# A layer of a hybrid decoder on one core: numbered banks in two lead-ins, another order of the cross attention, and four output weights split ahead

## The chip, the cores and the metric

The kernel runs on one core of a Trainium2 chip. The time is that of one execution on the device in microseconds; of several executions the median counts. Four compute engines work beside each other, each through its own queue in order: TensorE (PE in the profile) multiplies matrices into PSUM, which has eight banks of 512 fp32 values in each of 128 partitions; VectorE (DVE), ScalarE (ACT) and GpSimd (POOL) do the rest. SyncE (SP) issues nearly all DMA transfers. Semaphores order what the queues do.

## The reference, cut

One layer, 1024 tokens of 1024 features in fp32. First comes a token mixer (attention, a state-space branch, gates), then cross attention into 256 memory tokens, then a gated feed-forward network; each with an RMS norm before and after, added to the stream. What lies around the change:

```
h = rms_norm(x, g_pre_xa)
q = (h @ w_xq).reshape(bsz, seq, 4, 256)
k, v = split(mem_n @ w_xkv)                      # 256 memory tokens, 4 heads of 256
s = einsum('bshd,bmhd->bhsm', q, k) * 256 ** -0.5
p = softmax(s, axis=-1)
o = einsum('bhsm,bmhd->bshd', p, v).reshape(bsz, seq, 1024)
x = x + rms_norm(o @ w_xo, g_post_xa)
h = rms_norm(x, g_pre_ffn)
gate, up = split(h @ w_gu)                       # start of the feed-forward network
```

## The kernel before

Nearly every product is made of three: an operand is split into a high part, rounded to the fast fp32 format of TensorE, and the low part that is left, and `mm3` sums high x high, high x low and low x high. So a split costs one copy (`hi_sb`, on GpSimd or ScalarE in turn) and one subtraction (`lo_of`, on VectorE unless told otherwise).

The tokens are taken in two halves of 512 and in eight chunks of 128. The two big products h @ w_xq and h @ w_gu are made by a Strassen scheme on quadrants. `opening` (L1603) makes the first two products of such a scheme while the norm of the last row chunk still runs, in the banks of the pools psa (`bank`) and psx (`two_banks`, tile p). `lead_in` (L1619) goes on: `first_sum` on VectorE adds the first two products (into qT in the cross attention, into t in the feed-forward network), the pool psx is closed, and a pool psl with six banks opens in its place. Which of the six a tile gets is decided by the pool: all of them have the name mm. na[0] and na[1] are the next two products, banks[4:6] take the transposes of the last row chunk (`late.pop()`), pb the two after that.

The cross attention (L1790 to L1837) works on one chunk of 128 queries at a time in `soft`: scores of four heads into a tile p of two banks, a maximum (VectorE), four exponentials with their sums (ScalarE), reciprocal and multiplication (VectorE). `turn_(half, h)` transposes the probabilities of one head and four chunks (`tr`) and splits them (pTh on ScalarE, pTl on VectorE). `mix(half, h)` multiplies them with the values (xk holds these, split) into one of two banks, and splits the result (h). The loop turns a step ahead of the mix, and puts the scores of chunks 4 to 7 between the first mixes. In this part the program's own scheduler decides the order in each engine's queue.

`big_weight` fetches the eight row blocks k0 to k7 of w_xo into two rooms (wraw) and splits them into bw0 to bw7, once the queries (qT) are done. `out_proj` multiplies chunk by chunk with them (L125 to L127 of `mm3`, tile p), normalises, adds to the stream, and normalises again; a chunk's two banks become free when VectorE has read them (L1457).

A class `InTurn` (L34) stands before TensorE, VectorE and ScalarE: between `in_turn(True)` and `in_turn(False)` each instruction of such an engine is put behind the one before it in the code. Instructions recorded in that way all have the line L49. The lead-ins are inside such a stretch.

Of the kernel before, what the change touches and what calls it, by code (L numbers as in the profile page):

```python
# [54 lines left out]
def hybrid_block(ctx, tc, a, out, dbg=None):  # L55
# [1309 lines left out]
    def big_weight(wb, w, npool=0, raw_on_top=False):  # L1365
# [5 lines left out]
        first = [] if raw_on_top else [raw_room()]  # L1371
        rooms = {k: mk(wb, [P, 2, D], F32R, f"bw{k}", bufs=1) for k in reversed(range(KT))}
        for k in range(KT):
            raw = first.pop() if first else raw_room()
            nc.sync.dma_start(raw, w[k * P:(k + 1) * P, :])
            both = rooms[k]
            wh.append(both[:, 0, :])
            wl.append(both[:, 1, :])
            hi_sb(wh[k], raw, "p" if k < npool else None)
            lo_of(wl[k], raw, wh[k], G if k < npool else V)  # L1380
# [227 lines left out]
    def lead_in(hb, xf, pa, pb, q, nq, sfp, swp, y, n00, ny, last, nlast, open_ps, open_tx, loaded):  # L1608
# [56 lines left out]
        banks = [mk(psl, [P, HALF], F32, "mm") for _ in range(6)]  # L1665
# [64 lines left out]

    with ExitStack() as q2:
        qp = pool(q2, "qp", side="right")
        qP = [mk(qp, [P, 2, S], F32, f"qT{f}") for f in range(KT // 2)]
# [11 lines left out]
        with ExitStack() as xs:  # L1745
# [8 lines left out]
            def open_ps():  # L1754
                psx.close()
                return pool(psl, "psl", 6, PSUM)
# [15 lines left out]
            psx = ExitStack()  # L1772
            psp = pool(psx, "psx", 2, PSUM)
        pp = pool(q2, "pp", 4, side="right")
        prp = pool(q2, "prob", 6, side="right")
# [11 lines left out]

        sc = 256.0 ** -0.5
        prob = {}

        def soft(c):
            pt = prob[c] = mk(prp, [P, 4, ML], F32, "prob")
            mx = mk(stats, [P, 4], F32, "mx", bufs=4)
            sm_ = mk(stats, [P, 4], F32, "sm", bufs=4)
            pscr = mk(psp, [P, 4, ML], F32, "p2")
            for h in range(4):
                for k in range(2):
                    T.matmul(pscr[:, h, :], qT[2 * h + k][:, c * P:(c + 1) * P], kT[:, 2 * h + k, :], start=k == 0, stop=k == 1)  # L1798
            V.tensor_reduce(mx, pscr, mybir.AxisListType.X, ALU.max)
            V.tensor_scalar(mx, mx, -sc, None, ALU.mult)  # L1800
            for h in range(4):
                A.activation(pt[:, h, :], pscr[:, h, :], AF.Exp, scale=sc, bias=mx[:, h:h + 1], accum_out=sm_[:, h:h + 1])
            V.reciprocal(sm_, sm_)
            V.tensor_tensor(pt, pt, sm_.unsqueeze(2).to_broadcast([P, 4, ML]), ALU.mult)
# [3 lines left out]
        def turn_(half, h):  # L1808
            for mt in range(2):
                pt = mk(psp, [P, HALF], F32, "tr")  # L1810
                for ci in range(4):
                    T.transpose(pt[:, ci * P:(ci + 1) * P], prob[half * 4 + ci][:, h, mt * P:(mt + 1) * P], ident)
                hi, lo = mk(pp, [P, HALF], F32R, "pTh"), mk(pp, [P, HALF], F32R, "pTl")
                A.activation(hi, pt, AF.Copy)
                V.tensor_tensor(lo, pt, hi.bitcast(F32), ALU.subtract)
                pT[half, h, mt] = hi, lo

        def mix(half, h, out):
            for d in range(2):
# [4 lines left out]
                hi, lo = out[kk // 4]  # L1824
                A.activation(hi[:, kk % 4, :], po, AF.Copy)
                V.tensor_tensor(lo[:, kk % 4, :], po, hi[:, kk % 4, :].bitcast(F32), ALU.subtract)

        ox = [quad(h2, "h2"), quad(h2, "h2")]
        for c in range(4):
            soft(c)  # L1830
        steps = [(half, h) for half in range(2) for h in range(4)]
        turn_(0, 0)
        for i, (half, h) in enumerate(steps):
            if half == 0:
                soft(4 + h)
            if i + 1 < len(steps):
                turn_(*steps[i + 1])  # L1837
            mix(half, h, ox[half])

    q3, q3w = ExitStack(), ExitStack()  # L1840
    gpool = pool(q3, "gx3")
    wbig = pool(q3w, "wbigB", 8, side="right")
    wxo = big_weight(wbig, a["w_xo"][0], 2, True)
# [22 lines left out]
    with ExitStack() as q4:  # L1866
# [33 lines left out]
        def open_ps():  # L1900
            psx.close()
            return pool(psl, "psl", 6, PSUM)
# [299 lines left out]
```

## Time and profile before

| | |
|---|---|
| median of 3 runs | 2533.23 us (2532.54 to 2536.23) |
| profiled execution | 2529.46 us, span 2527.7 us |
| TensorE busy | 2452.0 us, 97% |
| VectorE, ScalarE, GpSimd busy | 1802.7, 1164.9, 818.6 us |
| mean granted TensorE clock | 0.996 |

The profile lists instructions with engine, line of the kernel, operation, and the tile that is written and those that are read. "[2.29 <-DVE qT L49]" behind a row says that its engine stood idle for 2.29 us before, and what ended that: an instruction of VectorE that writes qT, from line 49. A row of a timeline begins with its start and its length in microseconds; xN joins N neighbours. A matmul is shown with its whole passage through the array, so neighbours overlap, and their pace is read from their starts. PEld is the loading of weights into TensorE.

### The profile page before, as it was taken

To read this page: it belongs to the slowest core of one execution; us is meant where nothing else is said; L and a number is where in the kernel's file an instruction comes from. 1 tells how busy PE (TensorE), PEld (TensorE's weight loads), DVE (VectorE), ACT (ScalarE), POOL (GpSimd) and SP (SyncE) were. 2 spreads that over 40 slices of the span, in tenths; PEclk is the share of its full clock that TensorE was granted. 3 is DMA by queue.
4 is the path that set the end of the run, shared out by engine and by line. 5 is a ranking of instruction groups with operands and counts; after the bars stand their busy time and mean duration, and the time that the engine had idled before them with its cause. 6 is when DMAs were issued, how large, how long until landed. Compare 5 with 4: busy or idle time off the path is not lost. (4 is left out here: it accounts for less than half of the span.)

```text
span 2527.7 us, 33384 instructions
## 1 busy us (share of the span) xinstructions
PE 2452.0 (97%) x12306; PEld 2013.9 (80%) x12306; DVE 1802.7 (71%) x2165; ACT 1164.9 (46%) x2075; POOL 818.6 (32%) x638
## 2 busy tenths in 40 slices
PE   7999999999999999989999999999999999999998
PEld 5788888888788778877787778887788888888877
DVE  7765877767587877689889665566468555566997
ACT  5333455555456665566545313344335333334343
POOL 3221645443111211246556150101112322324662
PEclk9999999999999999999999999999999999999999
DMA  7441443333543444265332571321232323224232
GB/s 247 157 126 54 139 143 100 100 109 100 150 111 90 111 107 100 82 205 191 110 99 81 163 249 64 136 67 51 100 134 71 96 76 96 80 92 159 100 133 100
DMA packets 249133, 295.62 MB, mean 117 GB/s; under 512 B 17023, under 2 KB 169096, under 8 KB 248842
## 3 DMA queue, kind: packets, MB, share of 16 engines
q1 hardware_dynamic: 248682, 292.45, 37.0%
q8 instruction: 97, 1.59, 0.3%
q10 hardware_dynamic: 288, 1.05, 0.1%
q14 instruction: 66, 0.54, 0.1%
HBM read 202.20 MB, written 74.45 MB: 109 GB/s over the span
## 5 line engine op out<-in xcount | busy, mean ns | idle before, releaser
L911 DVE TENSOR_TENSOR_SCAN n<-n,mask 128x128 f32<-128x128 f32 (+7 forms) x128 | 189.8, 1509 | 23.8 <-ACT n L910 22.6
L122 DVE TENSOR_TENSOR sw<-sf,sw 128x512 fp32r<-128x512 f32 x142 | 127.4, 901 | 70.2 <-ACT sw L119 68.1
L119 ACT ACTIVATE sw<-sf 128x512 fp32r<-128x512 f32 x142 | 88.9, 628 | 155.8 <-PE mm L230 139.1
L928 ACT ACTIVATE wth<-tr,mone 128x512 fp32r<-128x512 f32 x192 | 110.7, 585 | 84.6 <-PE tr L925 82.6
L929 DVE SCALAR_TENSOR_TENSOR wtl<-tr,wth 128x512 fp32r<-128x512 f32 x192 | 99.6, 543 | 49.7 <-ACT wth L928 49.6
L196 POOL TENSOR_TENSOR sf<-wr,wr 128x512 f32<-128x512 f32 x36 | 52.4, 1455 | 235.5 <-DMA wr<-in_w_gu_dram 92.1
L693 DVE SCALAR_TENSOR_TENSOR b<-b,prmT,b 128x1023 f32<-128x1023 f32 (+2 forms) x72 | 109.6, 1522 | 16.9 <-ACT b L687 16.3
L122 DVE TENSOR_TENSOR sw<-wr,sw 128x512 fp32r<-128x512 f32 x107 | 100.1, 937 | 24.4 <-ACT sw L119 24.1
L115 POOL TENSOR_SCALAR v<-va 128x512 fp32r<-128x512 f32 x16 | 20.5, 1283 | 287.5 <-PE av L938 167.3
L229 PE MATMUL mm<-h,sw 128*128 128x512 f32 x288 | 112.0, 389 | 0.0
L230 PE MATMUL mm<-h,sw 128*128 128x512 f32 x288 | 111.7, 389 | 0.0
L228 PE MATMUL mm<-h,sw 128*128 128x512 f32 x288 | 109.9, 389 | 0.0
L910 ACT ACTIVATE n<-sc 128x512 f32<-128x512 f32 (+1 forms) x192 | 88.6, 494 | 46.1 <-PE tr L925 28.7
L173 POOL TENSOR_SCALAR rstd<-ms 128x1 f32<-128x1 f32 x74 | 29.2, 394 | 240.8 <-ACT x L180 164.6
L125 PE MATMUL mm<-oth,bw 128*128 128x512 f32 x256 | 104.3, 408 | 2.2 <-DVE a L1250 2.2
L125 PE MATMUL p<-bw,h 128*128 128x512 f32 x256 | 98.9, 392 | 2.4 <-DVE x L1457 2.4
L126 PE MATMUL mm<-otl,bw 128*128 128x512 f32 x256 | 101.2, 395 | 0.0
L127 PE MATMUL mm<-oth,bw 128*128 128x512 f32 x256 | 101.2, 395 | 0.0
L127 PE MATMUL p<-bw,h 128*128 128x512 f32 x256 | 100.2, 392 | 0.5 <-DVE h L122 0.5
L126 PE MATMUL p<-bw,h 128*128 128x512 f32 x256 | 100.0, 391 | 0.0
L925 PE MATMUL tr<-ident,n 128*128 128x128 f32 x576 | 95.4, 274 | 4.0 <-DVE wtl L929 4.0
L199 POOL TENSOR_TENSOR sf<-wr,sf 128x512 f32<-128x512 f32 x36 | 57.8, 1607 | 107.5 <-issue 85.6
(672 smaller groups left out, 7929.1 us busy)
## 6 DMA issues: line engine op xcount, KB each, us to landing
wr<-in_w_in_dram SPq DMA_DIRECT2D x36, 512.0 KB
wr<-in_w_gu_dram SPq DMA_DIRECT2D x72, 256.0 KB
zr<-in_w_in_dram SPq DMA_DIRECT2D x28, 512.0 KB
wraw<-in_w_in_dram SPq DMA_DIRECT2D x20, 512.0 KB
gu_d<-t SPq DMA_DIRECT2D x36, 256.0 KB
zs_d<-zo SPq DMA_DIRECT2D x32, 256.0 KB
xs_d<-b SPq DMA_DIRECT2D x32, 256.0 KB
kl<-gt SPq DMA_DIRECT2D x64, 128.0 KB
```

What stands on the lines that cost most here:

```text
L122: eng.tensor_tensor(o, i, hi.bitcast(F32), ALU.subtract)
L125: first = T.matmul(ps, sh, mh, start=start, stop=False)
L126: T.matmul(ps, sh, ml, start=False, stop=False)
L127: T.matmul(ps, sl, mh, start=False, stop=stop)
L228: T.matmul(ps, w[0][:, k, :], bh, start=first and k == 0, stop=False, skip_group_check=True)
L229: T.matmul(ps, w[0][:, k, :], bl, start=False, stop=False, skip_group_check=True)
L230: ins = T.matmul(ps, w[1][:, k, :], bh, start=False, stop=last and k == 3, skip_group_check=True)
L693: V.scalar_tensor_tensor(acc[:, sh:], y[:, :S - sh], cw(3 - sh, f), acc[:, sh:], ALU.mult, ALU.add)
L911: V.tensor_tensor_scan(nt[:, 0:L][:, ::-1], nt[:, 0:L][:, ::-1], mask[:, S - L:][:, ::-1], 1.0, ALU.mult, ALU.max)
L925: T.transpose(pt[:, tb * P:(tb + 1) * P], ns_[tb][:, i * P:(i + 1) * P], ident)
L928: A.activation(wh[:, t0 * P:], pt[:, t0 * P:], AF.Identity, bias=mone)
L929: V.scalar_tensor_tensor(wl[:, t0 * P:], pt[:, t0 * P:], -1.0, wh[:, t0 * P:].bitcast(F32), ALU.add, ALU.subtract)
```

## The change

- The six banks of both lead-ins have names of their own, mm0 to mm5, one buffer each.
- The cross attention is written in the order in which TensorE, VectorE and ScalarE are to take it, inside `in_turn(True)`. Scores go into four tiles of one bank (sc), two heads each. Probabilities have eight rooms, four tiles a8 of two chunks each. The multiplication with the reciprocal (`normed`) comes after the first half of the next chunk's maxima, or after a turn or a mix. Two turns are made ahead of the mixes; scores of chunks 6 and 7 stand between them. The split transposed probabilities live in tiles sw and pT.
- k0 to k3 of w_xo are fetched and split on GpSimd, high and low part, before the scores; k4 to k7 get the rooms of the queries and are split on ScalarE and VectorE after the last mix. The queries' pool lives on for them.
- `big_weight` loses two options that only w_xo used.

```diff
@@ -1362,13 +1362,13 @@
-    def big_weight(wb, w, npool=0, raw_on_top=False):
+    def big_weight(wb, w):
         wh, wl = [], []
...
-        first = [] if raw_on_top else [raw_room()]
+        first = [raw_room()]
         rooms = {k: mk(wb, [P, 2, D], F32R, f"bw{k}", bufs=1) for k in reversed(range(KT))}
@@ -1376,8 +1376,8 @@
             wl.append(both[:, 1, :])
-            hi_sb(wh[k], raw, "p" if k < npool else None)
-            lo_of(wl[k], raw, wh[k], G if k < npool else V)
+            hi_sb(wh[k], raw)
+            lo_of(wl[k], raw, wh[k])
         return wh, wl
@@ -1662,7 +1662,7 @@
         psl = open_ps()
-        banks = [mk(psl, [P, HALF], F32, "mm") for _ in range(6)]
+        banks = [mk(psl, [P, HALF], F32, f"mm{i}") for i in range(6)]
         pb, na = banks[0:2], banks[2:4]
@@ -1728,9 +1728,10 @@
+    q3w = ExitStack()
+    qp = pool(q3w, "qp", side="right")
     with ExitStack() as q2:
-        qp = pool(q2, "qp", side="right")
-        qP = [mk(qp, [P, 2, S], F32, f"qT{f}") for f in range(KT // 2)]
+        qP = [mk(qp, [P, 2, S], F32, f"bw{4 + f}") for f in range(KT // 2)]
         qT = [qP[f // 4 * 2 + f % 2][:, f % 4 // 2] for f in range(KT)]
@@ -1753,7 +1754,7 @@
                 psx.close()
-                return pool(psl, "psl", 6, PSUM)
+                return pool(psl, "psl", 1, PSUM)
@@ -1769,10 +1770,9 @@
             psl.close()
-            psx = ExitStack()
-            psp = pool(psx, "psx", 2, PSUM)
-        pp = pool(q2, "pp", 4, side="right")
-        prp = pool(q2, "prob", 6, side="right")
+        psm = pool(q2, "psm", 2, PSUM)
+        wbig = pool(q3w, "wbigB", 1, side="right")
+        ptp = pool(q2, "pT", 2)
         kT = mk(xk, [P, KT, ML], F32, "xk2")
@@ -1785,62 +1785,94 @@
+        wxo = [mk(wbig, [P, 2, D], F32R, f"bw{k}") for k in reversed(range(KT // 2))][::-1]
+
+        def xo_weight(k, hi_eng, lo_eng):
+            raw = mk(wbig, [P, D], F32, "wraw", 2)
+            nc.sync.dma_start(raw, a["w_xo"][0][k * P:(k + 1) * P, :])
+            hi_sb(wxo[k][:, 0], raw, hi_eng)
+            lo_of(wxo[k][:, 1], raw, wxo[k][:, 0], lo_eng)
+
+        for k in range(KT // 2):
+            xo_weight(k, "p", G)
+
         sc = 256.0 ** -0.5
-        prob = {}
+        pbt = [mk(accp, [P, 2, 4, ML], F32, "a8") for _ in range(NCH // 2)]
+        prob = [pbt[c // 2][:, c % 2] for c in range(NCH)]
+        sums, todo = {}, []
+
+        def normed():
+            while todo:
+                c = todo.pop()
+                V.reciprocal(sums[c], sums[c])
+                V.tensor_tensor(prob[c], prob[c], sums[c].unsqueeze(2).to_broadcast([P, 4, ML]), ALU.mult)
...
         def soft(c):
-            pt = prob[c] = mk(prp, [P, 4, ML], F32, "prob")
             mx = mk(stats, [P, 4], F32, "mx", bufs=4)
-            sm_ = mk(stats, [P, 4], F32, "sm", bufs=4)
-            pscr = mk(psp, [P, 4, ML], F32, "p2")
-            for h in range(4):
-                for k in range(2):
-                    T.matmul(pscr[:, h, :], qT[2 * h + k][:, c * P:(c + 1) * P], kT[:, 2 * h + k, :], start=k == 0, stop=k == 1)
-            V.tensor_reduce(mx, pscr, mybir.AxisListType.X, ALU.max)
-            V.tensor_scalar(mx, mx, -sc, None, ALU.mult)
-            for h in range(4):
-                A.activation(pt[:, h, :], pscr[:, h, :], AF.Exp, scale=sc, bias=mx[:, h:h + 1], accum_out=sm_[:, h:h + 1])
-            V.reciprocal(sm_, sm_)
-            V.tensor_tensor(pt, pt, sm_.unsqueeze(2).to_broadcast([P, 4, ML]), ALU.mult)
+            sums[c] = mk(stats, [P, 4], F32, "sm", bufs=4)
+            for h2 in range(2):
+                ps = mk(psm, [P, 2, ML], F32, "sc", 4)
+                for j in range(2):
+                    h = 2 * h2 + j
+                    for k in range(2):
+                        T.matmul(ps[:, j, :], qT[2 * h + k][:, c * P:(c + 1) * P], kT[:, 2 * h + k, :], start=k == 0, stop=k == 1)
+                m = mx[:, 2 * h2:2 * h2 + 2]
+                V.tensor_reduce(m, ps, mybir.AxisListType.X, ALU.max)
+                V.tensor_scalar(m, m, -sc, None, ALU.mult)
+                for j in range(2):
+                    h = 2 * h2 + j
+                    A.activation(prob[c][:, h, :], ps[:, j, :], AF.Exp, scale=sc, bias=mx[:, h:h + 1], accum_out=sums[c][:, h:h + 1])
+                if h2 == 0:
+                    normed()
+            todo.append(c)
...
             for mt in range(2):
-                pt = mk(psp, [P, HALF], F32, "tr")
+                pt = mk(psm, [P, HALF], F32, "tr")
                 for ci in range(4):
                     T.transpose(pt[:, ci * P:(ci + 1) * P], prob[half * 4 + ci][:, h, mt * P:(mt + 1) * P], ident)
-                hi, lo = mk(pp, [P, HALF], F32R, "pTh"), mk(pp, [P, HALF], F32R, "pTl")
-                A.activation(hi, pt, AF.Copy)
-                V.tensor_tensor(lo, pt, hi.bitcast(F32), ALU.subtract)
-                pT[half, h, mt] = hi, lo
-
-        def mix(half, h, out):
+                t = mk(ptp, [P, 2, HALF], F32R, "pT") if h % 2 else mk(ld, [P, 2, HALF], F32R, "sw")
+                A.activation(t[:, 0], pt, AF.Copy)
+                V.tensor_tensor(t[:, 1], pt, t[:, 0].bitcast(F32), ALU.subtract)
+                pT[half, h, mt] = t[:, 0], t[:, 1]
+            normed()
+
+        def mix(half, h):
             for d in range(2):
...
                     mm3(po, vh[mt][:, kk * P:(kk + 1) * P], vl[mt][:, kk * P:(kk + 1) * P], *pT[half, h, mt], mt == 0, mt == 1)
-                hi, lo = out[kk // 4]
+                hi, lo = ox[half][kk // 4]
                 A.activation(hi[:, kk % 4, :], po, AF.Copy)
                 V.tensor_tensor(lo[:, kk % 4, :], po, hi[:, kk % 4, :].bitcast(F32), ALU.subtract)
+                normed()
...
         ox = [quad(h2, "h2"), quad(h2, "h2")]
-        for c in range(4):
+        in_turn(True)
+        for c in range(6):
             soft(c)
+        turn_(0, 0)
+        soft(6)
+        turn_(0, 1)
+        soft(7)
         steps = [(half, h) for half in range(2) for h in range(4)]
-        turn_(0, 0)
-        for i, (half, h) in enumerate(steps):
-            if half == 0:
-                soft(4 + h)
-            if i + 1 < len(steps):
-                turn_(*steps[i + 1])
-            mix(half, h, ox[half])
-
-    q3, q3w = ExitStack(), ExitStack()
+        for i, step in enumerate(steps):
+            mix(*step)
+            if i + 2 < len(steps):
+                turn_(*steps[i + 2])
+        wxo += [mk(qp, [P, 2, D], F32R, f"bw{k}") for k in range(KT // 2, KT)]
+        for k in range(KT // 2, KT):
+            xo_weight(k, "a", V)
+        in_turn(False)
+    wxo = [w[:, 0] for w in wxo], [w[:, 1] for w in wxo]
+
+    q3 = ExitStack()
+    psx = ExitStack()
+    psp = pool(psx, "psx", 2, PSUM)
     gpool = pool(q3, "gx3")
-    wbig = pool(q3w, "wbigB", 8, side="right")
-    wxo = big_weight(wbig, a["w_xo"][0], 2, True)
     gpost, gpre = load_gain(gpool, "g_post_xa"), load_gain(gpool, "g_pre_ffn")
@@ -1899,7 +1931,7 @@
             psx.close()
-            return pool(psl, "psl", 6, PSUM)
+            return pool(psl, "psl", 1, PSUM)
```

VectorE's queue, where the first mixes of the cross attention and the last multiplications of probabilities stand, before (pTl: low part of transposed probabilities; h: that of a mix's result; sm: sums of a chunk; prob: its probabilities):

```order
L1826 TENSOR_TENSOR h_3200_15963<-mm_16162,h_3199_15962 128x512
L1826 TENSOR_TENSOR h_3200_15963<-mm_16171,h_3199_15962 128x512
L1815 TENSOR_TENSOR pTl_16206<-tr_16200,pTh_16205 128x512
L1803 RECIPROCAL sm_16182<-sm_16182 128x4
L1804 TENSOR_TENSOR prob_16180<-prob_16180,sm_16182 128x1024
L1815 TENSOR_TENSOR pTl_16215<-tr_16209,pTh_16214 128x512
L1803 RECIPROCAL sm_16238<-sm_16238 128x4
L1804 TENSOR_TENSOR prob_16236<-prob_16236,sm_16238 128x1024
L1826 TENSOR_TENSOR h_3202_15965<-mm_16218,h_3201_15964 128x512
L1826 TENSOR_TENSOR h_3202_15965<-mm_16227,h_3201_15964 128x512
L1815 TENSOR_TENSOR pTl_16262<-tr_16256,pTh_16261 128x512
L1815 TENSOR_TENSOR pTl_16271<-tr_16265,pTh_16270 128x512
```

and with the change (pT and sw: transposed probabilities, a: probabilities, sc: scores, h: result of a mix):

```order
L49 TENSOR_TENSOR pT_16167<-tr_16162,pT_16167 128x512
L49 TENSOR_TENSOR pT_16175<-tr_16170,pT_16175 128x512
L49 RECIPROCAL sm_16143<-sm_16143 128x4
L49 TENSOR_TENSOR a_3210_15985<-a_3210_15985,sm_16143 128x1024
L49 TENSOR_REDUCE mx_16180<-sc_16182 128x2
L49 TENSOR_SCALAR mx_16180<-mx_16180 128x2
L49 TENSOR_REDUCE mx_16180<-sc_16191 128x2
L49 TENSOR_SCALAR mx_16180<-mx_16180 128x2
L49 TENSOR_TENSOR h_3212_15987<-mm_16200,h_3211_15986 128x512
L49 RECIPROCAL sm_16181<-sm_16181 128x4
L49 TENSOR_TENSOR a_3210_15985<-a_3210_15985,sm_16181 128x1024
L49 TENSOR_TENSOR h_3212_15987<-mm_16211,h_3211_15986 128x512
```

Before, the maxima of all chunks are behind it and low parts of mixes stand on both sides of the two multiplications. Now the first low part of a mix, written from mm_16200, stands behind the multiplication of one chunk and the maxima of the next.

TensorE's queue where the scores end, before (p: scores of chunk 7 in one tile, tr: transposes, mm: a mix):

```order
L1798 MATMUL p_3268_16239<-xk_3194_15950,qT_3135_15415 128x256
L1798 MATMUL p_3268_16239<-xk_3194_15950,qT_3134_15414 128x256
L1798 MATMUL p_3268_16239<-xk_3194_15950,qT_3135_15415 128x256
L1812 MATMUL tr_16144<-ident_88,prob_15970 128x128
L1812 MATMUL tr_16144<-ident_88,prob_15990 128x128
L1812 MATMUL tr_16144<-ident_88,prob_16010 128x128
L1812 MATMUL tr_16144<-ident_88,prob_16030 128x128
L1812 MATMUL tr_16153<-ident_88,prob_15970 128x128
L1812 MATMUL tr_16153<-ident_88,prob_15990 128x128
L1812 MATMUL tr_16153<-ident_88,prob_16010 128x128
L1812 MATMUL tr_16153<-ident_88,prob_16030 128x128
L125 MATMUL mm_16162<-pTh_16093,xk_3196_15954 128x512
```

and with the change (bw: here still the queries, in the rooms that k4 to k7 get later):

```order
L49 MATMUL sc_16191<-xk_3194_15950,bw_3134_15414 128x256
L49 MATMUL sc_16191<-xk_3194_15950,bw_3135_15415 128x256
L49 MATMUL mm_16200<-sw_16129,xk_3196_15954 128x512 x3
L49 MATMUL mm_16200<-sw_16137,xk_3198_15959 128x512 x3
L49 MATMUL mm_16211<-sw_16129,xk_3196_15954 128x512 x3
L49 MATMUL mm_16211<-sw_16137,xk_3198_15959 128x512 x3
L49 MATMUL tr_16220<-ident_88,a_3207_15982 128x128 x2
L49 MATMUL tr_16220<-ident_88,a_3208_15983 128x128 x2
L49 MATMUL tr_16228<-ident_88,a_3207_15982 128x128 x2
L49 MATMUL tr_16228<-ident_88,a_3208_15983 128x128 x2
L49 MATMUL mm_16236<-pT_16167,xk_3196_15954 128x512 x3
L49 MATMUL mm_16236<-pT_16175,xk_3198_15959 128x512 x3
```

Before, a turn follows the last scores, and the mix behind it is that of a turn made earlier. Now the first mix follows the last scores, then comes a turn, and mm_16236 is the third bank asked of two.

The last matmuls of the first two row chunks of the output projection on TensorE before (p_3329 is chunk 0, p_3336 chunk 1, p_3345 chunk 2):

```order
L125 MATMUL p_3329_16479<-bw_3303_16427,h_3201_15964 128x512
L126 MATMUL p_3329_16479<-bw_3303_16427,h_3201_15964 128x512
L127 MATMUL p_3329_16479<-bw_3303_16427,h_3202_15965 128x512
L126 MATMUL p_3336_16545<-bw_3303_16427,h_3201_15964 128x512
L127 MATMUL p_3336_16545<-bw_3303_16427,h_3202_15965 128x512
L125 MATMUL p_3336_16545<-bw_3303_16427,h_3201_15964 128x512
L126 MATMUL p_3336_16545<-bw_3303_16427,h_3201_15964 128x512
L127 MATMUL p_3336_16545<-bw_3303_16427,h_3202_15965 128x512
L125 MATMUL p_3345_16627<-bw_3310_16434,h_3199_15962 128x512
```

and with the change (p_3317, p_3324, p_3333):

```order
L126 MATMUL p_3317_16482<-bw_3302_16445,h_3213_15988 128x512
L127 MATMUL p_3317_16482<-bw_3302_16445,h_3214_15989 128x512
L126 MATMUL p_3324_16548<-bw_3301_16444,h_3213_15988 128x512
L127 MATMUL p_3324_16548<-bw_3301_16444,h_3214_15989 128x512
L125 MATMUL p_3324_16548<-bw_3302_16445,h_3213_15988 128x512
L126 MATMUL p_3324_16548<-bw_3302_16445,h_3213_15988 128x512
L127 MATMUL p_3324_16548<-bw_3302_16445,h_3214_15989 128x512
L125 MATMUL p_3324_16548<-bw_3302_16445,h_3213_15988 128x512
L126 MATMUL p_3324_16548<-bw_3302_16445,h_3213_15988 128x512
L127 MATMUL p_3324_16548<-bw_3302_16445,h_3214_15989 128x512
L125 MATMUL p_3333_16630<-bw_3202_15965,h_3211_15986 128x512
```

Chunk 0 ended five matmuls before the first of chunk 2, and now ends eight before it.

## The prediction

> **What bounds the kernel now.** I read the page first, then the waits of TensorE over the whole span, then its timeline round the two places that the diff touches, and last the queues of VectorE and ScalarE there.
>
> ```profile
> span 2527.7 us, 33384 instructions
> PE 2452.0 (97%) x12306; PEld 2013.9 (80%) x12306; DVE 1802.7 (71%) x2165; ACT 1164.9 (46%) x2075; POOL 818.6 (32%) x638
> ```
>
> TensorE is busy for 97% of the span, so only what makes it wait or slows it can move the end: the stretch from the first lead-in to the end of the second is worth what TensorE loses there. The profiled execution took 2529.46 us, 3.8 us under the median of 2533.23; losses are counted in the profiled one and the difference is taken off the median.
>
> ```profile
> PE p L125 <- DVE x L1457: 2.4, 1, 2.4
> PE tr L1812 <- DVE prob L1804: 2.3, 2, 1.4
> ...
> PE mm L49 <- DVE qT L49: 2.3, 1, 2.3
> ...
> PE mm L49 <- DVE t L49: 2.2, 1, 2.2
> ```
>
> These are four of TensorE's waits, each in a place that the change reaches: the two lead-ins (qT, t), the cross attention (prob) and the third row chunk of its output projection (x). The timeline of TensorE at the lead-ins:
>
> ```profile
> 1638.09 2.88 PE L49 MATMUL p<-a,wraw 128*128 128x512 f32 x12
> 1643.26 3.06 PE L49 MATMUL mm<-a,sw 128*128 128x512 f32 x12 [2.29 <-DVE qT L49]
> ...
> 1877.54 2.88 PE L49 MATMUL p<-a,wraw 128*128 128x512 f32 x12
> 1882.59 3.02 PE L49 MATMUL mm<-a,sw 128*128 128x512 f32 x12 [2.17 <-DVE t L49]
> ```
>
> A matmul of 512 columns is listed with 0.39 us but they follow each other faster: twelve take 2.88, so (2.88 - 0.39)/11 = 0.227 from start to start. By starts, the first lead-in loses 5.17 - 12 x 0.227 = 2.45 us and the second 5.05 - 2.72 = 2.33.
>
> **The lead-in banks.** The matmuls into mm (na[0], L1667) wait for VectorE's first_sum, the last reader of the PSUM bank that the pool hands them. With numbered banks, na[0] takes the bank mm2, which is another one; its last reader is the normalisation of the stream:
>
> ```profile
> 1635.23 1.28 DVE L49 SCALAR_TENSOR_TENSOR x<-p,rstd,g_post_mix 128x1024 f32<-128x1024 f32 x1 [1.31 <-POOL rstd L174]
> ...
> 1640.12 1.28 DVE L49 SCALAR_TENSOR_TENSOR x<-x,rstd,g_pre_xa 128x1024 f32<-128x1024 f32 x1
> ...
> 1642.52 0.68 DVE L49 TENSOR_TENSOR qT<-qT,p 128x512 f32<-128x512 f32 x1
> ...
> 1646.79 0.69 DVE L49 TENSOR_TENSOR x<-mm,xk 128x512 f32<-128x512 f32 x1 [2.99 <-PE mm L49]
> ```
>
> The first row ends at 1636.5, long before 1640.8, when TensorE is free. What is late next: after na[0] come eight transposes of x, whose input (second row) is there at 1641.4; they would start at 1640.8 + 2.7 = 1643.5. VectorE sits idle for 2.99 us before it reads their result, so it moves forward with them. The bank that first_sum holds goes to mm1, which is first written after the transposes and na[1], past 1646, while first_sum (third row) ends at 1643.2. So I take the whole: **-4.78 us** for both. The bounds are 0, if another operand comes in late, and this sum.
>
> **The cross attention.** TensorE from the first score to the first matmul of the output projection:
>
> ```profile
> 1712.49 10.88 PE L1798 MATMUL p<-xk,qT 128*128 128x256 f32 x48
> 1723.21 0.38 PE L1812 MATMUL tr<-ident,prob 128*128 128x128 f32 x2
> 1724.23 3.72 PE L1798 MATMUL p<-xk,qT 128*128 128x256 f32 x16 [0.64 <-ACT prob L1802]
> ...
> 1753.35 0.38 PE L1812 MATMUL tr<-ident,prob 128*128 128x128 f32 x2
> 1755.12 0.30 PE L1812 MATMUL tr<-ident,prob 128*128 128x128 f32 x1 [1.40 <-DVE prob L1804]
> 1755.63 0.55 PE L1812 MATMUL tr<-ident,prob 128*128 128x128 f32 x3 [0.21 <-DVE pTl L1815]
> 1757.10 0.41 PE L1812 MATMUL tr<-ident,prob 128*128 128x128 f32 x2 [0.92 <-DVE prob L1804]
> ...
> 1758.99 0.63 PE L126 MATMUL mm<-pTl,xk 128*128 128x512 f32 x1
> ...
> 1761.55 0.44 PE L126 MATMUL mm<-pTl,xk 128*128 128x512 f32 x1
> ...
> 1762.06 1.04 PE L1812 MATMUL tr<-ident,prob 128*128 128x128 f32 x8
> ...
> 1765.68 1.03 PE L1812 MATMUL tr<-ident,prob 128*128 128x128 f32 x8
> ...
> 1776.00 0.62 PE L125 MATMUL p<-bw,h 128*128 128x512 f32 x2
> ```
>
> Three chunks of scores take 1723.21 - 1712.49 = 10.72, so 3.57 each; a turn with a mix (eight transposes and twelve matmuls) takes 1765.68 - 1762.06 = 3.62. Eight of each are 57.5 us without any loss; measured are 1776.00 - 1712.49 = 63.5. So **6.0 us** are lost, the most that a new order can win here. The waits make 3.9 of it by starts: 0.8 before 1724.23 and 3.1 between 1753.35 and 1757.6. Then the matmuls run slowly: six from 1758.99 to 1761.55 are 0.427 apart, 1.2 us over their pace, with some 0.4 more on both sides: 1.6 us. The rest is restarts.
>
> After the change, scores have four single banks, probabilities eight rooms, and normalisation comes later, so the old waits go (the rooms of prob were six, and chunks 6 and 7 waited behind them). But VectorE's and ScalarE's queues are now in the order of the code, and there stands, between the scores of chunk 6 and the first result of a mix, one whole round of both engines for each of chunks 6 and 7. Its terms are in rows of before:
>
> ```profile
> 1727.13 1.22 DVE L1804 TENSOR_TENSOR prob<-prob,sm 128x1024 f32<-128x1024 f32 x1
> 1728.27 1.22 DVE L1799 TENSOR_REDUCE mx<-p 128x4 f32<-128x1024 f32 x1
> 1729.53 0.17 DVE L1800 TENSOR_SCALAR mx<-mx 128x4 f32<-128x4 f32 x1
> ...
> 1737.66 1.28 DVE L1815 TENSOR_TENSOR pTl<-tr,pTh 128x512 fp32r<-128x512 f32 x2
> ```
> ```profile
> 1729.79 0.47 ACT L1802 ACTIVATE prob<-p,mx 128x256 f32<-128x256 f32 x1 [2.90 <-DVE mx L1800]
> ...
> 1730.25 0.47 ACT L1802 ACTIVATE prob<-p,mx 128x256 f32<-128x256 f32 x1
> ...
> 1735.64 1.08 ACT L1814 ACTIVATE pTh<-tr 128x512 fp32r<-128x512 f32 x2 [0.50 <-PE tr L1812]
> ```
>
> A round: two low halves 1.2, reciprocal and multiplication 0.2 + 1.14, a maximum over half as much 0.63 (an estimate, half of 1728.27 to 1729.53), the scaling to the first exponential 0.26, four exponentials at 0.46 = 1.84, a copy of 0.6: 5.9 us, after which VectorE may write the next low half. TensorE needs only 0.9 + 3.57 = 4.5 in that time. Let S be the end of chunk 5's scores on TensorE. VectorE is then still multiplying for 0.6; maximum, scaling, two exponentials and a copy make 2.4, so the first low half starts at S + 3.0, the one of the first mix result two rounds later at S + 14.8, and it ends at S + 15.5. That is what the first matmul of mix(0,1) waits for, since banks for results are two. TensorE gets there at S + 0.9 + 3.57 + 0.9 + 3.57 + 2.72 + 0.9 = S + 12.6. I take 3.2 us of waiting, between 2.9 and, with some 0.1 for each of four handovers, 3.3. The second half of mix(0,1) waits again: the low half of mix(0,0)'s second result stands behind one more multiplication and ends at 14.8 + 0.6 + 1.34 + 0.69 = S + 17.4, TensorE is there 0.55 earlier. From there each step has four low halves, 2.4 us of VectorE against 3.62 of TensorE: no more waits. Together 3.75 us.
>
> Whether the slow clock comes too decides 1.6 us:
>
> ```profile
> 1240.00:1250.00 10.00, 8.28 (x55) 6.27 (x55) 8.51 (x10) 4.80 (x10) 6.79 (x8) 0.83 0.56 161
> ```
> ```profile
> 1640.00:1650.00 10.00, 7.71 (x39) 6.11 (x38) 6.64 (x11) 3.13 (x6) 0.00 (x0) 1.00 0.35 105
> ```
> ```profile
> 1750.00:1760.00 10.00, 7.37 (x35) 5.54 (x33) 7.63 (x11) 7.21 (x23) 9.47 (x5) 0.91 0.26 87
> ```
>
> In these slices (first number after the length: TensorE busy; third from the end: granted clock) 1.72 us of idle time gave 0.83, 2.29 gave 1.00, and 2.63 gave 0.91. A stall of over 3 us is longer than all three, so I count the dip in, at two chances in three. The Trainium skill, "TensorE: Matmul & The Clock Gate", Part 1, says that the clock is halved after at least one idle window of about 3.4 us; by that rule a stall of 3.2 us brings no dip. This trace does not agree: the clock fell after 1.72 us. With the dip the loss is 3.75 + 1.6 = 5.35 instead of 6.0: **-0.65 us**.
>
> **Output projection and its weights.**
>
> ```profile
> 1797.53 0.39 PE L127 MATMUL p<-bw,h 128*128 128x512 f32 x1
> 1800.33 0.50 PE L125 MATMUL p<-bw,h 128*128 128x512 f32 x1 [2.41 <-DVE x L1457]
> ```
>
> Chunk 2 waits until chunk 0's sum has been normalised: 2.80 - 0.23 = 2.57 us. Chunk 0 ended five matmuls before chunk 1; in the new order it ends eight before, three more to cover the same chain: 3 x 0.227 = **-0.68 us**.
>
> Of the weights:
>
> ```profile
> 1751.50 2.39 POOL L122 TENSOR_TENSOR bw<-wraw,bw 128x1024 fp32r<-128x1024 f32 x1
> ```
> ```profile
> 1785.03 1.23 DVE L122 TENSOR_TENSOR bw<-wraw,bw 128x1024 fp32r<-128x1024 f32 x1 [0.52 <-ACT bw L119]
> ```
> ```profile
> 1791.89 1.06 ACT L119 ACTIVATE bw<-wraw 128x1024 fp32r<-128x1024 f32 x1 [6.89 <-DMA wraw<-in_w_xo_dram]
> ```
>
> k0 to k3 are split on GpSimd from about 1697, when the last query weights are done, at some 4 us each, and are needed past 1765: hidden. k4 to k7 are split when the last mix has ended (E). raw6 can be fetched when k4's low half is done, at about E + 2.8, raw7 1.2 later. In before, raw7 was fetched when 1785.03 + 1.23 = 1786.26 was over and was there at 1791.89, 5.6 us later: the worst of this place. So raw7 is there at E + 9.7 at the latest, its low half 2.3 later, at E + 12. TensorE has 27 matmuls before the first of k4 and 63 before the low half of k7: E + 14.3. The two gain vectors (512 KB each) are now queued on SP ahead of raw6, behind the last reader of the room; that is in the way of the 2 us left. I count nothing, and 3 us at the other end.
>
> **Sum.** 4.78 + 0.65 + 0.68 = 6.1: 2533.2 - 6.1 = **2527.1 us**. A measurement of this kernel can tell about 0.2%, 5.1 us, from no change; the forecast is just past it.
>
> **Rivals.**
> - *The stall without the dip* (chance 0.24; the forecast itself 0.46): 1.6 us more is won, 2525.5. For it: 2.29 us at 1640 left the clock alone.
> - *No stall* (0.04): VectorE keeps up. Then all of 6.0 goes: -11.5, 2521.7. Against it: 5.9 against 4.5 per round.
> - *The banks do not do what they say* (0.12): another operand of the lead-ins is as late, and of 4.78 nothing or half comes: 2532 to 2529.5. For it: VectorE works without a gap up to the end of first_sum at 1643.2. Against: its next row waits for TensorE.
> - *Late weights* (0.08): raw6 and raw7 queue behind the gains; up to 3 us of waiting before k6 and k7: 2530.
> - *Slower* (0.06): VectorE never catches up, since the order is forced: each of the six mixes after the first two takes a round of 5.9 instead of 3.62: +13.7, 2541. It decides if VectorE has more than 3.62 us of work per step. Against it: 2.4 us by the rows above.
>
> **Numbers.** Faster by over 0.2% are two thirds of the forecast's case (its terms are uncertain by 2 us), nearly all of the second, and the third: 0.59. Slower is the last and a little beside it: 0.07. The rest, 0.34, is within 0.2%. The range 2523.0 to 2531.5 leaves out the third and the last case and half of the fourth.
>
> **What would show it.** In the new profile: no wait for DVE qT or t at the lead-ins; first score near 1710.1; one TensorE wait of about 3 us for DVE in the first matmul of the second mix, one of 0.5 after it; granted clock below 1 in that slice; no wait for bw; chunk 2 waiting 1.8 instead of 2.4. A wait for bw or x over 2 us, or waits in every mix, would make me wrong.

## The result and the profile after

The changed kernel takes 2532.14 us (median of 12 runs, 2528.83 to 2535.28), the kernel before 2535.71 in the runs beside it (12 runs, 2532.54 to 2539.98). The ratio is 0.9983 with a 95% interval of 0.9975 to 0.9991: between 2.3 and 6.3 us less. 6.1 us were forecast; by the prediction's own bound of 0.2% this is still "no change". As a plain time 2532.14 lies above the forecast range (2523.0 to 2531.5), but before was also slower beside it than in the runs that the forecast started from (2533.23): 3.6 us off that is 2529.6. The profiled execution of the changed kernel has a span of 2528.0 us, no shorter than before's 2527.7: it lost 3.8 us ahead of the part that was changed (the p of the first lead-in starts at 1641.88 instead of 1638.09), where the two programs are the same. So from here on I compare stretches between the same two events in each trace, and not spans.

TensorE's waits in the changed kernel between 1600 and 1910 us (engine, line, what it waited for: us in total, times, the longest):

```profile
PE mm L49 <- DVE h L49: 3.7, 1, 3.7
PE mm L49 <- DVE x L49: 3.3, 1, 3.3
PE p L125 <- DVE x L1457: 1.7, 1, 1.7
PE tr L49 <- DVE sw L49: 1.0, 1, 1.0
PE mm L49 <- DVE sw L49: 0.2, 1, 0.2
```

The waits for qT, t and prob are gone. In their place stand one for h in the cross attention, forecast, and one for x and two smaller ones for sw, not forecast. TensorE's timeline at the two lead-ins:

```profile
1641.88 2.88 PE L49 MATMUL p<-a,wraw 128*128 128x512 f32 x12
1644.60 2.89 PE L49 MATMUL mm<-a,sw 128*128 128x512 f32 x12
1647.33 1.03 PE L49 MATMUL mm<-ident,x 128*128 128x128 f32 x8
...
1878.01 2.88 PE L49 MATMUL p<-a,wraw 128*128 128x512 f32 x12
1880.73 2.88 PE L49 MATMUL mm<-a,sw 128*128 128x512 f32 x12
1886.88 1.06 PE L49 MATMUL mm<-ident,x 128*128 128x128 f32 x8 [3.27 <-DVE x L49]
1887.70 7.53 PE L49 MATMUL mm<-a,sw 128*128 128x512 f32 x32
```

In both, na[0] now follows p at once. In the first the transposes do too. In the second they wait 3.27 us for x. VectorE's timeline there, and SyncE's:

```profile
1877.66 1.28 DVE L49 SCALAR_TENSOR_TENSOR x<-p,rstd,g_post_xa 128x1024 f32<-128x1024 f32 x1 [1.19 <-POOL rstd L174]
1881.88 1.23 DVE L49 TENSOR_TENSOR x<-x,x 128x1024 f32<-128x1024 f32 x1 [2.94 <-DMA x<-x_d]
```
```profile
1870.51 0.37 SPq L1578 DMA_DIRECT2D fg<-in_w_gu_dram  x1
...
1873.55 1.17 SPq L1453 DMA_DIRECT2D x<-x_d  x1
```

The same two rows of SyncE in before:

```profile
1860.98 0.37 SPq L1578 DMA_DIRECT2D fg<-in_w_gu_dram  x1
...
1867.13 1.20 SPq L1453 DMA_DIRECT2D x<-x_d  x1
```

The stream's last row chunk (x<-x_d) is fetched behind five transfers for the feed-forward network, and the first of these (fg) is issued 9.5 us later than before. Against the start of p (1878.01 and 1877.54) x is issued 4.5 us ahead instead of 10.4; VectorE waits 2.94 us for it, and the whole norm behind it is late. The reason is memory: fg lies where the queries' pool was. That pool now lives on as k4 to k7, so under fg lies k6, which the last row chunk of the output projection reads nearly to its end; before, k0 lay there. The traces bear this out. In the changed kernel SyncE waits for the projection's matmuls ahead of fg:

```profile
SPq L1578 <- PE p L127: 14.6, 1, 14.6
```

The last row chunk has 48 matmuls, six for each weight. fg is issued just behind the 42nd, the last of k6, which starts at 1870.09; in before, just behind the sixth, the last of k0, which starts at 1860.57.

The stretches, in us, each from starts of rows on TensorE: "lead-in 1" from its p to the first score, "attention" from there to chunk 2 of the output projection, "projection" from there to the p of lead-in 2, "lead-in 2" from there to the first product behind its transposes.

| kernel | lead-in 1 | attention | projection | lead-in 2 | sum |
|---|---|---|---|---|---|
| before | 74.40 | 87.84 | 77.21 | 8.70 | 248.15 |
| changed | 71.78 | 87.12 | 77.23 | 9.69 | 245.82 |
| e1: before, banks numbered | 71.77 | 88.02 | 77.22 | 6.23 | 243.24 |
| e2: changed, banks as before | 76.63 | 87.41 | 77.24 | 15.92 | 257.20 |
| e3: changed, order of weights | 71.77 | 86.99 | 77.21 | 6.23 | 242.20 |
| e4: changed, k0 to k3 split late | 71.78 | 85.66 | 77.21 | 8.96 | 243.61 |
| e5: changed, mix(0, 0) first | 71.78 | 87.15 | 77.21 | 8.99 | 245.13 |
| e6: e3, e4 and e5 together | 71.81 | 86.95 | 77.21 | 6.23 | 242.20 |
| e7: e3 and e5 together | 71.77 | 87.16 | 77.21 | 6.23 | 242.37 |
| e8: e6, last softmax in two pieces | 71.77 | 87.15 | 77.22 | 6.23 | 242.37 |
| e9: before once more | 74.74 | 88.00 | 77.21 | 10.38 | 250.33 |
| e10: changed once more | 71.80 | 87.08 | 77.21 | 9.91 | 246.00 |

In the cross attention of the changed kernel, VectorE while the first scores run (GpSimd's timeline of the same time behind it), and then the two low halves on which the prediction's sum rests:

```profile
1716.31 1.86 DVE L49 TENSOR_SCALAR mx<-mx 128x2 f32<-128x2 f32 x1
...
1719.94 1.82 DVE L49 TENSOR_SCALAR mx<-mx 128x2 f32<-128x2 f32 x1
...
1739.09 1.29 DVE L49 TENSOR_TENSOR sw<-tr,sw 128x512 fp32r<-128x512 f32 x2 [1.64 <-ACT sw L49]
...
1751.09 0.69 DVE L49 TENSOR_TENSOR h<-mm,h 128x512 fp32r<-128x512 f32 x1 [1.77 <-ACT h L49]
```
```profile
1715.80 2.35 POOL L122 TENSOR_TENSOR bw<-wraw,bw 128x1024 fp32r<-128x1024 f32 x1
...
1719.38 2.35 POOL L122 TENSOR_TENSOR bw<-wraw,bw 128x1024 fp32r<-128x1024 f32 x1
```

A scaling of two numbers in each partition, mostly 0.17 us, takes 1.86 and ends at 1718.17, as GpSimd's subtraction ends (1718.15); the other ends at 1721.76, GpSimd's at 1721.73. The Trainium skill, "SBUF — State Buffer", section "Who interferes with whom", says that a tensor_scalar on VectorE, in its modes with two ports, can hold or be held by GpSimd at a shared pair of ports, and that the second to issue waits until the first is done. The times of these rows agree; which mode the scaling ran in they do not show.

TensorE in the changed kernel, from the turn behind chunk 5's scores on, and the slice with the granted clock (third number from the end):

```profile
1734.38 1.04 PE L49 MATMUL tr<-ident,a 128*128 128x128 f32 x8
...
1739.83 0.44 PE L49 MATMUL tr<-ident,a 128*128 128x128 f32 x2 [0.96 <-DVE sw L49]
```
```profile
1747.15 1.03 PE L49 MATMUL tr<-ident,a 128*128 128x128 f32 x8
1751.84 4.63 PE L49 MATMUL mm<-pT,xk 128*128 128x512 f32 x12 [3.66 <-DVE h L49]
1756.31 1.03 PE L49 MATMUL tr<-ident,a 128*128 128x128 f32 x8
```
```profile
1750.00:1760.00 10.00, 8.16 (x33) 6.62 (x34) 6.97 (x11) 5.30 (x13) 0.00 (x0) 0.83 0.00 0
```

So S, the end of chunk 5's scores, is 1734.38. The first low half starts at S + 4.7, that of the first mix result two rounds of 6.0 later. TensorE waits 0.96 and 3.66 us, and the next twelve matmuls take 4.47 instead of 2.72, at a clock of 0.83. Chunk 2 of the projection waits 1.73 us instead of 2.41.

### The profile page after: what moved, and what is told of

Its sections match the earlier page's. It is cut to its first block, busy times and chain, and to the rows that moved or that the text cites. A ratio compares the mean times of both kernels' runs of the same rounds, so it can differ in the third digit from the quotient of the medians.

```text
span 2528.0 us, 33414 instructions
## 1 busy us (share of the span) xinstructions
PE 2450.5 (97%) x12306; PEld 2015.0 (80%) x12306; DVE 1809.3 (72%) x2179; ACT 1166.4 (46%) x2076; POOL 821.4 (32%) x639
## 5 line engine op out<-in xcount | busy, mean ns | idle before, releaser
L119 ACT ACTIVATE zh<-zr 128x512 fp32r<-128x512 f32 x72 | 45.0, 630 | 104.8 <-PE ma L492 52.3
```

What stands on the lines that cost most here:

```text
L119: A.activation(o, i, AF.Copy)
```

## The experiments

All are variants of one of the two kernels, timed against before in five rounds, but for the last two.

**e1: only the banks are numbered.** An edit of the kernel before, in both lead-ins (each pool of six buffers also becomes one of one buffer per name):

```diff
-        banks = [mk(psl, [P, HALF], F32, "mm") for _ in range(6)]
+        banks = [mk(psl, [P, HALF], F32, f"mm{i}") for i in range(6)]
```

> The kernel before with the six lead-in banks numbered and nothing else changed. Theory (the second lead-in lost its gain because the room of fg moved under a late reader, which is not so here): no wait of TensorE for VectorE above 0.4 us in either lead-in, and 2.4 + 2.3 = 4.8 us less than before (ratio 0.998). Rival (the numbered banks themselves only hand the wait of the second lead-in on to the transposes): the first lead-in gains 2.5, the second waits about 3 us for x as in the changed kernel, 1.6 us less than before in all.

2526.12 us, ratio 0.9965 (0.9953 to 0.9978). TensorE in the second lead-in:

```profile
1878.30 2.89 PE L49 MATMUL mm<-a,sw 128*128 128x512 f32 x12
1881.02 1.03 PE L49 MATMUL mm<-ident,x 128*128 128x128 f32 x8
```

No wait is left in either lead-in: the numbered banks do all that the prediction claimed, 2.6 and 2.5 us by the table. They hand no wait on; the wait for x is made by another part of the change. By the stretch the banks alone (243.24) are 2.6 us ahead of the whole change (245.82): what the new cross attention gains, the second lead-in loses, and more. The whole time fell by more than the stretch, 5.6 to 11.9 us against 4.9; e9 comes back to this.

**e2: the change without the numbered banks.** The edit of e1, backwards, in the changed kernel.

> The changed kernel with the banks of both lead-ins named mm as before. Theory: the cross attention alone is worth 0.7 us; fg is still fetched 9 us late, so VectorE is late in the second lead-in, and now the matmuls wait for first_sum instead of the transposes for x: about 8 us of wait there against 2.2 before. 5 us slower than before. Rival (fg has nothing to do with it): both lead-ins wait 2.2 us as before, 0.7 us faster than before.

2542.11 us, ratio 1.0026 (1.0016 to 1.0036): slower than before. The second lead-in:

```profile
1894.55 0.79 PE L49 MATMUL mm<-a,sw 128*128 128x512 f32 x1 [7.10 <-DVE t L49]
```

As the theory had it: the late x now holds up first_sum too, and na[0] waits 7.1 us for that. With the slow matmuls behind it the second lead-in takes 15.92 us instead of 8.70; attention gains 0.4 here. Not in the theory is the first lead-in: its wait is 2.96 us here, with slow matmuls behind it, and it takes 76.63 instead of 74.40. The cross attention and the weights, as they are written, are a loss without the banks.

In the second mix this execution shows something that the changed kernel's trace does not, in one mix of two halves of six matmuls:

```profile
1758.05 1.67 PE L49 MATMUL mm<-pT,xk 128*128 128x512 f32 x6 [3.66 <-DVE h L49]
1759.99 2.93 PE L49 MATMUL mm<-pT,xk 128*128 128x512 f32 x6 [0.28 <-DVE h L49]
```

The wait of 3.66 is the same, but the first six matmuls still run at full pace, and the second six then wait 0.28 us, before they run slowly.

**e3: the last row chunk takes k6, k5, k4, k7 first.**

```diff
-            for k in range(KT):
+            ks = order if held else tuple(range(KT))
+            for k in ks:
...
-    out_proj(1, ox[1], wxo, t4, psp, x2_d, x3_d, gpost, gpre, second_half(hw, xf), lead_gu)
+    out_proj(1, ox[1], wxo, t4, psp, x2_d, x3_d, gpost, gpre, second_half(hw, xf), lead_gu, (6, 5, 4, 7, 0, 1, 2, 3))
```

> The changed kernel, but the last row chunk of the output projection takes the weights in the order k6, k5, k4, k7, k0 to k3, so that the room under fg is read for the last time early. Theory: fg is fetched near 1862 instead of 1870.5 (in the changed kernel's time), x of the last chunk lands before it is needed, the wait of 3.3 us in the second lead-in goes, 3.4 us less than the changed kernel, 7 less than before (ratio 0.997). Rival (x was late by chance of the transfers in one execution): nothing changes, 3.6 us less than before.

2526.74 us, ratio 0.9967 (0.9955 to 0.9978). SyncE and TensorE:

```profile
1859.77 0.37 SPq L1579 DMA_DIRECT2D fg<-in_w_gu_dram  x1
...
1866.31 0.34 SPq L1453 DMA_DIRECT2D x<-x_d  x1
```
```profile
1879.04 2.89 PE L49 MATMUL mm<-a,sw 128*128 128x512 f32 x12
1881.76 1.03 PE L49 MATMUL mm<-ident,x 128*128 128x128 f32 x8
```

fg is issued 16.6 us ahead of p (1876.32), as in before, and the wait for x is gone: 9.69 to 6.23 us. Nothing but the order of eight weights in one row chunk was changed, so the late readers of fg's room are what cost the 3.5 us.

**e4: k0 to k3 are split behind the scores.** A write of one column by ScalarE behind chunk 7's exponentials holds back the two first fetches.

```diff
-        for k in range(KT // 2):
-            xo_weight(k, "p", G)
...
         soft(7)
+        for k in range(KT // 2):
+            xo_weight(k, "p", G, sums[7][:, 0:1] if k < 2 else None)
```

> The changed kernel, but k0 to k3 of w_xo are fetched and split on GpSimd after the scores instead of beside the first ones. Theory (VectorE's small scalings, 1.9 and 1.8 us instead of 0.17, were held by GpSimd's splits and left VectorE 1.6 to 2.2 us late for the rest of the scores): all scalings take 0.17 us, VectorE is idle between chunks, the wait of 1.0 us before the second turn goes and that before the second mix is 2 to 3 us instead of 3.7; 1.7 to 2.5 us less than the changed kernel. Rival (the wait is made by the order of the queues alone): 3.7 and 1.0 us of wait as before, no gain.

2528.21 us, ratio 0.9975 (0.9965 to 0.9986). VectorE, and TensorE:

```profile
1713.91 0.17 DVE L49 TENSOR_SCALAR mx<-mx 128x2 f32<-128x2 f32 x1
...
1735.13 1.29 DVE L49 TENSOR_TENSOR sw<-tr,sw 128x512 fp32r<-128x512 f32 x2 [1.64 <-ACT sw L49]
```
```profile
1731.98 1.04 PE L49 MATMUL tr<-ident,a 128*128 128x128 f32 x8
...
1736.31 1.04 PE L49 MATMUL tr<-ident,a 128*128 128x128 f32 x8
...
1748.07 4.58 PE L49 MATMUL mm<-pT,xk 128*128 128x512 f32 x12 [3.62 <-DVE h L49]
```

Theory and rival each hold for one of the two waits. The scalings take 0.17 us, the first low half starts at S + 3.15 (1735.13 - 1731.98), and the wait of 0.96 before the second turn is gone; attention takes 85.66 us, 1.46 less. But 3.62 us of wait before the second mix stay. GpSimd's splits cost 1 to 1.5 us; the large wait is the order's alone.

**e5: mix(0, 0) ahead of the scores of chunk 7.**

```diff
         turn_(0, 1)
+        mix(0, 0)
         soft(7)
...
-            mix(*step)
+            if i:
+                mix(*step)
```

> The changed kernel, but mix(0, 0) is written ahead of the scores of chunk 7 instead of behind them. Theory (the wait of 3.7 us before the second mix is one whole round of VectorE and ScalarE that stands between the first result and its low part): the low part of the first mix now stands ahead of chunk 7's maxima, the 3.7 us go, of which 1 to 2 us come back before the third mix or its turn; the slow clock behind it goes or is shorter. 3 to 4 us less than the changed kernel. Rival (VectorE and ScalarE have too much work in all, and TensorE waits for it wherever it stands): the wait moves to the third mix in full, no gain.

2529.58 us, ratio 0.998 (0.997 to 0.9989). TensorE:

```profile
1751.70 1.25 PE L49 MATMUL tr<-ident,a 128*128 128x128 f32 x8 [1.61 <-DVE sw L49]
1754.24 4.53 PE L49 MATMUL mm<-sw,xk 128*128 128x512 f32 x12 [1.28 <-DVE h L49]
```

Here the rival is right as to the time, though the wait moves to more than the third mix. The wait of 3.66 before the second mix is down to 0.21, but 1.61 and 1.28 stand before the next turn and the next mix, with the slow clock behind them. Attention takes 87.15 us, as without the edit.

**e6 and e7: edits together.** e6 has those of e3, e4 and e5, e7 those of e3 and e5.

> The changed kernel with three edits at once: the order of weights in the last row chunk (k6, k5, k4, k7 first), k0 to k3 split after the scores, mix(0, 0) ahead of the scores of chunk 7. Theory: the gains add up to 3.4 + 1.0 + 4.5 = 8.9 us less than the changed kernel by the traces, and it is faster than the kernel before with the numbered banks alone by about 6. Rival (the splits of k0 to k3 collide with other work when the scores end sooner, or the weights are late): 4 to 5 us less than the changed kernel, with waits for bw or for DVE in the mixes.

> As the last one, but k0 to k3 are split beside the first scores as in the changed kernel. Theory: VectorE is 1.6 us late at the end of chunk 5's scores, so that 1 us of wait stands before the second turn and the others follow: 1 to 2 us more than with the splits after the scores. Rival (the order has slack for it): the same time within 0.5 us.

e6: 2524.71 us, ratio 0.9961 (0.9948 to 0.9973). e7: 2523.07 us, ratio 0.9952 (0.9938 to 0.9966), the best of all here. The intervals overlap, and by the stretches (242.20 and 242.37) neither is better than e3 alone. So in e6 the gains of e3 came in full, those of e4 and e5 did not add. "About 6 faster than with the numbered banks alone" was wrong; by the stretches it is 1.0. The theory of e7, 1 to 2 us more than e6, was wrong too: by the stretch it is 0.2. The wait of 0.93 us before the second turn is there in e7 and gone in e6, as that theory had it, but the third mix takes it back, in e6 (first row) against e7:

```profile
1750.15 5.49 PE L49 MATMUL mm<-sw,xk 128*128 128x512 f32 x12 [1.28 <-DVE h L49]
```
```profile
1754.94 4.62 PE L49 MATMUL mm<-sw,xk 128*128 128x512 f32 x12 [1.28 <-DVE h L49]
```

The waits around it are nearly the same (1.82 and 1.65 before its turn), but the slow clock lasts longer in e6: 0.70 on average from 1750 to 1760, against 0.83 in e7. Whether that is the order or the chance of one execution was not tested.

**e8: chunk 7's softmax in two pieces.** As e6, with

```diff
+        scores(7)
+        turn_(0, 2)
+        part(7, 0)
+        mix(0, 1)
+        turn_(0, 3)
+        part(7, 1)
...
+        mix(0, 2)
+        mix(0, 3)
+        turn_(1, 0)
```

> As the kernel with three edits (k6, k5, k4, k7 first in the last row chunk; k0 to k3 split after the scores; mix(0, 0) ahead of the scores of chunk 7), but the softmax of chunk 7 is cut in two halves: the scores are made in one go, the first half's maxima and exponentials stand behind the turn (0, 2), the second half's behind the turn (0, 3), and later turns are made one step ahead of their mix. Theory (what waits is never the amount of work but a whole softmax that stands in one piece between a result and its low part): no wait of TensorE above 1.5 us in the mixes, no slow clock; 3 to 4 us less than with the three edits. Rival (VectorE and ScalarE have the work of a softmax and four splits per step to do in any case): waits of 3 us in all somewhere in the mixes, the same time within 1 us.

2525.89 us, ratio 0.997 (0.9959 to 0.998); attention 87.15 us. TensorE:

```profile
1749.09 3.03 PE L49 MATMUL mm<-sw,xk 128*128 128x512 f32 x12 [0.96 <-DVE h L49]
...
1754.13 4.61 PE L49 MATMUL mm<-pT,xk 128*128 128x512 f32 x12 [2.01 <-DVE h L49]
...
1760.75 1.25 PE L49 MATMUL tr<-ident,a 128*128 128x128 f32 x8 [1.14 <-DVE sw L49]
```

The waits are 0.96, 2.01 and 1.14, 4.1 us in all, against 3.1 in e6, and behind the second the twelve matmuls run slowly (4.61): the theory of one piece in the wrong place falls, and the time is the rival's, within 1 us. The orders tried leave 3.1 to 4.6 us of waiting in the cross attention, each in other places. What they share is that a softmax, two copies of a turn and two of a mix have to go through ScalarE and VectorE in turn, each waiting for the other, while TensorE has no more scores to fill the time. That this alone makes the amount was not shown by an edit of its own.

**e9 and e10: both kernels profiled again.**

> The kernel before, unchanged, profiled once more, to see how far the stretch from the first lead-in's p to the second lead-in's end differs between executions (248.2 us in the first profile). Theory (what the experiments gain in this stretch is less than in the whole time, since the first profile of before happened to be a quick one outside it): 248.2 within 0.5 us, and a longer time ahead of it or behind it. Rival (the first profile was quick within the stretch): 250 us or more.

> The changed kernel, unchanged, profiled once more. Theory (fg is fetched late by the order of its room's readers, not by chance): the second lead-in waits again for x, by 2.5 to 3.5 us, and the stretch takes 245.8 within 0.7 us. Rival (chance of the transfers): a wait under 1.5 us or over 5.

The changed kernel repeats itself: 246.00 us, 2.72 us of wait for x. Before does not, and the rival is right: it takes 250.33. TensorE in its second lead-in:

```profile
1885.62 4.45 PE L49 MATMUL mm<-a,sw 128*128 128x512 f32 x12 [2.24 <-DVE t L49]
1889.87 1.26 PE L49 MATMUL mm<-ident,x 128*128 128x128 f32 x8
```

The same wait of 2.2 us is followed here by twelve matmuls in 4.25 us instead of 2.86: the slow clock, which the first profile showed in neither lead-in. The two profiles of before have four such waits, 2.17 to 2.67 us long; each costs itself, and one of the four 1.4 to 1.7 us more.

The two profiles of the changed kernel show the same. Here is the second lead-in's wait for x in e10, and the slices with the granted clock from 1880 to 1890, first of the changed kernel's first profile, then of e10:

```profile
1884.20 1.94 PE L49 MATMUL mm<-ident,x 128*128 128x128 f32 x8 [2.72 <-DVE x L49]
```
```profile
1880.00:1890.00 10.00, 6.73 (x34) 5.41 (x34) 8.12 (x12) 3.50 (x7) 0.79 (x2) 1.00 0.48 179
```
```profile
1880.00:1890.00 10.00, 7.28 (x31) 5.99 (x30) 10.00 (x17) 5.43 (x10) 0.79 (x2) 0.83 0.27 102
```

The longer wait of 3.27 us left the clock at 1.00, and the eight transposes behind it take 1.06; the shorter one of 2.72 was followed by the slow clock, and they take 1.94.

So the gain of the banks can be larger than the first profile shows, by an estimate of up to some 3 us if both waits bring the slow clock. The granted clocks of the timed runs point the same way. On average they are 0.9945 in the 20 runs of before that stand beside e1, and 0.9957 in e1's six. As an estimate, 0.0012 of 2530 us is 3 us lost to the slow clock; e1's whole time gained 4.0 us more than its stretch. For e7 (0.9972 against 0.9949) it is 5.9 us, with 5.5 gained beyond the stretch. So a large part of what the whole times gained beyond the stretches is probably slow clock; at which places, the runs do not show. A single pair of spans tells little: the span up to the first p alone, the same code in all twelve profiles, is between 1637.8 and 1643.3 us.

## Why the prediction was right in direction, and where it was wrong

Less time was forecast, and less it took, 3.6 us for 6.1. The prediction gave 0.59 to more than 0.2% and 0.34 to what came, a change within it. Its own sign of being wrong, "a wait for bw or x over 2 us", is there: 3.27 us for x in the second lead-in. The sum by its stretches, in the first two profiles:

- **First lead-in**: -2.45 forecast, -2.62 measured. Right, step by step.
- **Second lead-in**: -2.33 forecast, +0.99 measured. The wait for t went, as the step said, and e1 shows the full gain where nothing else is changed. The step that failed is "what is late next". The eight transposes were to start at once behind na[0]; they waited 3.27 us. The prediction took the time of x from the trace of before, and went through banks and engines; it did not ask which room the queries' pool had left to the feed-forward network, now that it lives on. The order of the weights' readers then sets the issue of fg, and with it x, which is behind it on SyncE. The rival "the banks do not do what they say" gave 0.12 to a late operand, with a time (2532 to 2529.5) that fits what was measured, but its mechanism was not this one: e1 shows no wait with the banks alone, so the late operand comes from the room, not from the banks.
- **Cross attention with chunk 2**: -1.33 forecast, -0.72 measured. Place and kind of the wait were right: the second mix, for the low half of the first, one round of 5.9 forecast and 6.0 measured. Mis-sized was "VectorE is then still multiplying for 0.6": scalings were held by GpSimd, that multiplication ended at S + 2.3, and the first low half stood at S + 4.7, not at S + 3.0. e4, without the hold, has S + 3.15. What remains of the sum is a wait of 3.62 for 3.2. The second wait of 0.55 did not come in the changed kernel, since the slow matmuls gave VectorE the time: in e2, where the first six ran at full pace, it is there with 0.28.
- **The slow clock** came, as forecast, at 1.75 us for 1.6. The rival without it is out for waits as long as those that came: it followed each of the five before the second mix, 3.62 to 3.67 us (the changed kernel, e2, e3, e4, e10). For a wait of the length forecast, 2.9 to 3.3 us, it is not shown; behind the 3.27 us of the second lead-in the clock stayed at 1.00. That the wait was longer than forecast may have helped, and that is luck. The rule of the Trainium skill that the prediction cites ("TensorE: Matmul & The Clock Gate", Part 1, an idle window of about 3.4 us) fits these six waits. It does not fit the slow clock behind 2.24 us in e9 and 2.72 in e10, and the measurement decides.
- **Output projection**: chunk 2 waits 0.68 less, as forecast, and no weight was late.
- **The rivals** of late weights, of no stall, and of a slower loop are not seen: TensorE has no wait for a weight in the projection, and none from the third mix on.

Together these come to 2.3 us, not 6.1; the missing gain in the second lead-in is 3.3 of the difference. By e9 and e10 the stretch gains 4.3, mostly because before had the slow clock behind one of its waits there. No term of the forecast held that, so as far as it made up for the second lead-in, the sum came near by luck.

## What to carry to other kernels

When a pool lives longer, or a tile takes over another's room, list who gets the memory next, which reader frees it, and what stands behind that fetch on its queue; here the order of eight weights was worth 3.5 us. When a wait is removed, follow the operands of the next instruction to their transfers, and not only to the engine that writes them. When work is moved to GpSimd to hide it, look at what VectorE does at that time: even a scaling of 0.17 us can be held until GpSimd's instruction ends.

## What the runs showed of the hardware that was not expected

A scaling of 128x2 numbers on VectorE took 1.86 us instead of 0.17, up to the end of GpSimd's subtraction; with GpSimd's splits moved away (e4) it took 0.17. And the same wait in the same place of the same program was followed by a slow clock in one execution and by none in another: in before 2.24 us with it and 2.17 without, in the changed kernel 2.72 with it and 3.27 without. So a trace with none is no evidence that a wait is cheap.
